# Seven products in place of eight for 31 more weight units, sums formed inside the weight buffer, and a planner that waits for whole PSUM tiles

## The chip, the cores and the metric

The kernel runs on one core of a Trainium2 chip. The metric is device microseconds of one execution, the median of several. Five engines work side by side: PE (matmuls and transposes), DVE (element-wise work on two inputs), ACT (casts, activations, copies), POOL (hardly used here) and SP, which issues the DMAs that bring the weights in.

## The reference, cut to what matters

One layer of a streaming encoder on 256 tokens of 2048 features; every large step is a product of a 256-row activation with a weight matrix read once from HBM.

```python
x = x + 0.5 * swiglu(rms_norm(x, ffn1_norm), w_gate, w_up, w_down)   # 2048 -> 5632 -> 2048
h = rms_norm(x, mix_norm); u, q, k, v, g, a = split(h @ w_in)
x = x + concat(pool_mixer(u), gated_linear_attention(q, k, v, g, a)) @ w_out
x = x + cross_attention(rms_norm(x), rms_norm(mem))                  # w_q, w_kv, then @ w_o
x = x + 0.5 * swiglu(rms_norm(x, ffn2_norm), w_gate2, w_up2, w_down2)
out = rms_norm(x) * final_norm
```

## The kernel before

**Units.** The weights come in 378 units of 1 MB (`load`, a tile `raw` of 128 x 2048 f32). Each value is split into a rounded part and the rest, so that fast matmuls keep f32 accuracy: ACT casts `raw` to `wh`, DVE subtracts to get `wl` (`split`). Activations are kept split in the same way (`xs` for the normalised input, `ys` for hidden or attention outputs). A product of two split numbers takes three matmuls: high by high, high by low, low by high.

**A plain unit** (`unit_p`, `block_t`) holds two k tiles by two column blocks of 512, and has two token halves: 8 products of three matmuls, 24 matmuls of 128 x 128 x 512. **A seven unit** (`split_seven`, `seven`) forms the same 2 x 2 block product with 7 products in Strassen's manner (21 matmuls). For that it needs sums of activation tiles (`part_sums`, once for each pair of k tiles and reused by every block; they go to `xe`), sums of the four weight pieces (DVE), a second cast and subtraction for the pieces that stand alone (`xh`, `xl`, 128 x 1536), and after the last seven unit of a block a few DVE and ACT operations that put the partial products together (`combine`, then `join`).

**Blocks.** A block is 8 units (6 for the shorter down products) that accumulate into PSUM tiles `pt`. PSUM holds four tiles of two banks each. A plain block (`block_t`) uses two tiles, a block with seven units (`block_s`) four: two hold products that `combine` reads, two the sums that `join` reads.

**Stages.** Each feed-forward network (`ffn`) runs in three parts (`FF_PARTS`): gate and up blocks (32, 32 and 24 units), transposes of the hidden rows (`turn`, tile `ph`), then the down product into x (`into_x`; 16, 16 and 12 units). Before the change seven units are used in gate and up blocks alone, at `PAIRS` (0, 2, 4, 6) of each 8, except in the very first gate block of each network: 80 units. The down products, `w_out` and `w_o` are plain, and so is the last part of the second down product (`down_end`), before and after.

**What sets the order.** The code records operations; `Plan` then gives each an estimated cost and a latest start, and lists them engine by engine (`schedule`); each engine runs its list in that order. The recorder tracks which parts of a tile an operation touches in cells of 64 elements (`grain`), so the planner takes the two banks of a PSUM tile to be independent, while the tile framework that emits the semaphores makes a writer wait for earlier readers of the whole PSUM tile. `Stream.emit` splits weights ahead of PE: by one unit for the first four units, by two after (`AHEAD`); `wh` and `wl` have three buffers, `xh` and `xl` two, `raw` three (`RAW`). The sums of weights go to a tile `T` of their own, with one buffer for each stage.

In the profile nearly every instruction has the line of the recorder's call (L469), so groups are told apart by their tiles.

Of the kernel before, what the change touches and what calls it, by code (L numbers as in the profile page):

```python
# [36 lines left out]
class Stream:  # L37
# [7 lines left out]
    RAW = 3  # L45
    FIRST = 4
# [15 lines left out]
    def unit(self, load, f, split=None, prepare=None):  # L62
        self.items.append((len(self.units), f))
        self.units.append((load, split, prepare))
        self.pending = [(n - 1, h) for n, h in self.pending]
        self._flush()

    def emit(self, load, prepare, split):
        done, w, late = -1, {}, []
        for u, f in self.items:  # L70
            if u is None:
                f()
                continue
            ahead = 1 if u < self.FIRST else self.AHEAD
            while done < min(u + ahead, len(self.units) - 1):
                done += 1
                while late:
                    late.pop(0)()
                if done + 1 < len(self.units):
                    prepare(done + 1, self.units[done + 1][2])  # L80
                w[done], rest = split(done, self.units[done][1])

                def finish(done=done, rest=rest):
                    if rest:
                        rest()
                    if done + self.RAW < len(self.units):
                        load(done + self.RAW)

                if rest:
                    late.append(finish)  # L90
                else:
                    finish()
            f(*w.pop(u))


def cost(engine, name, args, kw, writes, reads):
# [12 lines left out]
    if engine == "scalar":  # L109
# [5 lines left out]
        if "accum_out" in kw:  # L115
            busy += 0.1
# [10 lines left out]
class Buf:  # L127


    def __init__(self, shape, make, scope=None, psum=False, dtype=None):  # L130
# [6 lines left out]
        self.grain = 1 if n <= 128 else 64  # L137
# [72 lines left out]
class Task:  # L210
    __slots__ = ("i", "engine", "run", "busy", "tail", "moved", "preds", "succs", "start", "late",
                 "table", "what")
# [7 lines left out]
class Plan:  # L220
# [61 lines left out]
    def touch(self, t, v, write):  # L282
# [3 lines left out]
        b.users.append(t)  # L286
        for c in v.cells():
            spans = b.cells.setdefault(c, [])
            keep = []
            for s in spans:  # L290
                p0, p1, wrote, u = s
                if p0 < v.p1 and v.p0 < p1:
                    if write or wrote:
                        self.dep(t, u, wrote)
                    if write and v.p0 <= p0 and p1 <= v.p1:
                        continue
                keep.append(s)
            keep.append((v.p0, v.p1, write, t))
# [37 lines left out]
    def latest(self):  # L336
# [17 lines left out]
        for t in reversed(order):  # L354
            late = -t.busy - t.tail
            for s in t.succs:
                if t.engine is None:
                    x = s.late
                elif t.moved:
                    x = s.late - 1.8 - t.moved / 338e3  # L360
# [9 lines left out]
    def schedule(self):  # L370
# [47 lines left out]
        while any(waiting.values()):  # L418
# [7 lines left out]
            busy = t.busy  # L426
# [5 lines left out]
            if t.moved:  # L432
                wire = max(wire, at + 1.8) + t.moved / 338e3
# [8 lines left out]
    WAIT = 0.2  # L442

# [9 lines left out]
class Recorder:  # L453
# [3 lines left out]
    def __getattr__(self, name):  # L457
        def call(*args, **kw):
# [12 lines left out]
            t = plan.add(e, run, **cost(e, name, args, kw, writes, reads))  # L471
            t.what = (name, [v.buf.name for v in writes], [v.buf.name for v in reads])
# [8 lines left out]
def build(ctx, tc, I, out):  # L481
# [142 lines left out]
    def finish_norm(n, spread_too=True):  # L624
# [3 lines left out]
        if spread_too:  # L628
            diag["R"] = [diagonal(Rcol[:, t : t + 1]) for t in range(2)]
# [87 lines left out]
    def part_sums(act, ext, i, g):  # L717

        t = local([P, 4 * NB], F32, tag="T", name=uid("T"))
        a = t[:, :NB].rearrange("p (k s) -> p k s", k=2)  # L720
        e = t[:, NB : 2 * NB].rearrange("p (n s) -> p n s", n=4)
# [4 lines left out]
        a11, a21, a12, a22 = (a[:, k, h * P : (h + 1) * P] for k in range(2) for h in range(2))  # L726
        nc.vector.tensor_tensor(out=e[:, 3], in0=a11, in1=a21, op=ALU.subtract)
        nc.vector.tensor_tensor(out=e[:, 1], in0=a22, in1=a21, op=ALU.subtract)
        nc.vector.scalar_tensor_tensor(
            out=e[:, 2], in0=e[:, 1], scalar=-1.0, in1=a11, op0=ALU.mult, op1=ALU.subtract  # L730
        )
        nc.vector.tensor_tensor(out=e[:, 0], in0=a12, in1=e[:, 2], op=ALU.add)
        split(ext[:, i, 0], ext[:, i, 1], e)

    def add_weights(u, raw):
        t = local([P, 4 * NB], F32, tag="T", name=f"T{u}")
        w = raw.rearrange("p (b n) -> p b n", n=NB)
        v = t.rearrange("p (b n) -> p b n", n=NB)
        nc.vector.tensor_tensor(
            out=v[:, 0:2], in0=w[:, 1:3], in1=w[:, 0:1].to_broadcast([P, 2, NB]), op=ALU.add  # L740
        )
        nc.vector.tensor_tensor(out=v[:, 2], in0=v[:, 0], in1=w[:, 2], op=ALU.add)
        nc.vector.tensor_tensor(out=v[:, 3], in0=v[:, 2], in1=w[:, 3], op=ALU.add)
        return t

    def split_seven(u, raw, t):
        th, tl = (
            tile_of(wpool, [P, 4 * NB], F32R, tag=n, name=f"{n}{u}", bufs=st.AHEAD + 1)
            for n in ("wh", "wl")
        )  # L750
        split(th, tl, t)
        parts = [x.rearrange("p (b n) -> p b n", n=NB) for x in (th, tl)]

        if True:
            r = [
                local([P, 3 * NB], F32R, tag=n, name=f"{n}{u}", bufs=2)
                for n in ("xh", "xl")
            ]
            split(*r, raw[:, NB:])
            parts.extend(x.rearrange("p (b n) -> p b n", n=NB) for x in r)  # L760

        return [parts], None

    def seven(banks, act, ext, i, g, first, later, weights):
        th, tl, rh, rl = weights
        k0, k1, lo, hi = 2 * g, 2 * g + 1, slice(0, P), slice(P, S)
        a11, a12, a22 = ([act[:, k, p, t] for p in range(2)] for k, t in ((k0, lo), (k1, lo), (k1, hi)))
        n4, n1, s2, s3 = ([ext[:, i, p, n] for p in range(2)] for n in range(4))
        table = {
            "P1": (a11, rh[:, 0], rl[:, 0]), "P3": (n4, rh[:, 1], rl[:, 1]),  # L770
            "P2": (a12, rh[:, 2], rl[:, 2]), "P5": (n1, th[:, 0], tl[:, 0]),
            "P7": (s3, th[:, 1], tl[:, 1]), "P6": (s2, th[:, 2], tl[:, 2]),
            "P4": (a22, th[:, 3], tl[:, 3]),
# [3 lines left out]
        for n in order:  # L777
            (a, b), wh, wl = table[n]
            for j, (x, w) in enumerate(((a, wh), (a, wl), (b, wh))):
                nc.tensor.matmul(  # L780
                    banks[n], x, w, start=first and j == 0,
                    stop=not later and n in ("P1", "P5", "P6", "P7") and j == 2,
                )

    def block_s(srcs, act, ext, pairs, evict, delays=(0, 0), joins=(1, 0)):

        held, n = {}, len(srcs)

        def open_banks():
            a, b, c, d = (ptile(uid("pt")) for _ in range(4))  # L790
            held["ps"] = (d, c)
            held["parts"] = (a, b)
            held["banks"] = {
                "P1": a[:, 0], "P6": a[:, 1], "P7": b[:, 0], "P5": b[:, 1],
                "P2": c[:, 0], "P4": c[:, 1], "P3": d[:, 0],
            }

        def unit_s(g):
            def fn(weights):
                if g == pairs[0]:  # L800
                    open_banks()
                seven(held["banks"], act, ext, pairs.index(g), g, g == pairs[0], g != pairs[-1],
                      weights)
            return fn

        def unit_p(g):
            def fn(wh, wl):
                wh, wl = (w.rearrange("p (k j n) -> p k j n", j=2, n=NB) for w in (wh, wl))
# [3 lines left out]

# [876 lines left out]
```

## Time and profile before

| | us |
|---|---|
| median of three runs (2136.68 to 2138.38) | 2136.95 |
| the profiled execution's own time | 2133.25 |
| its span, first to last instruction | 2131.5 |
| mean granted TensorE clock | 0.997 |

How to read it: "busy" is the time in which an engine had at least one instruction under way; "idle before" and "waits" say how long an engine stood still ahead of an instruction, and who released it. Consecutive instructions of DVE and ACT overlap slightly, so the distance from one start to the next is a better price than the length of one. A stage is cut out with a window from the span's start: the second gate and up stage of the first network is 275 to 441 us, the down product after it 441 to 530, `w_o` 1324 to 1421, the first gate and up stage of the second network 1421 to 1587.

### The profile page before, as it was taken

The page shows a single profiled execution, that of the slowest core. Times are in us where ns is not written, and L with a number is a line of the kernel's source. Part 1 is how long each engine was busy: PE and PEld are TensorE (multiplying, and loading weights), DVE is VectorE, ACT ScalarE, POOL GpSimd, SP SyncE. Part 2 cuts the span into 40 slices and gives each one's busy share as a digit, 9 for nine tenths or more (in the row PEclk, how much of TensorE's full clock was granted, in tenths as well). Part 3 has the DMA queues.
Part 4 walks back from the last instruction along what each step waited for, and adds up shares of the span by engine and source line. Part 5 has one row for each costly group of instructions (what it writes and reads, how often), then busy time and mean ns, then how long its engine had stood idle before and what let it go on. Part 6 is the DMA issues. An engine that isn't in the chain of part 4 may idle for free.

```text
span 2131.5 us, 24136 instructions
## 1 busy us (share of the span) xinstructions
PE 2101.8 (99%) x9954; PEld 1754.1 (82%) x9954; DVE 1551.7 (73%) x1315; ACT 1041.7 (49%) x918; POOL 15.8 (1%) x41
## 2 busy tenths in 40 slices
PE   8999999999999999899999999999999999999998
PEld 6888888888888888788888888888888888888886
DVE  7997599966996577565556554568994899758974
ACT  6554355533554555346444444445553455435543
POOL 0000000000000000000000000000000000000001
PEclk9999999999999999999999999999999999999999
DMA  7557656566666655467655555665567655766673
GB/s 250 199 185 255 221 201 210 196 237 217 214 204 239 213 161 184 132 192 282 224 191 159 173 162 162 212 198 197 197 214 235 222 198 186 248 217 217 197 257 119
DMA packets 143318, 435.93 MB, mean 205 GB/s; under 512 B 9828, under 2 KB 13000, under 8 KB 142824
## 3 DMA queue, kind: packets, MB, share of 16 engines
q1 hardware_dynamic: 143176, 434.38, 61.0%
q8 instruction: 78, 1.28, 0.2%
q14 instruction: 32, 0.26, 0.0%
q10 hardware_dynamic: 32, 0.01, 0.0%
HBM read 417.58 MB, written 16.78 MB: 204 GB/s over the span
## 4 chain that ended last, share of the span: by engine, by line
PE 84%; DVE 9%; ACT 3%; issue 2%; DMA 2%; SPq 0%; DVEq 0%; ACTq 0%
PE pt L469 57%; PE pa L469 15%; PE pb L469 6%; DVE wl L469 4%; PE pe L469 3%; DVE T L469 2%; ACT wh L469 2%; DVE sg L469 2%; PE ph L469 1%; DVE xl L469 1%; DMA raw<-in_ffn_w_gate 1%; PE pv L469 1%; PE pl L469 1%; PE px L469 1%; DMA raw<-in_ffn_w_up 0%
## 5 line engine op out<-in xcount | busy, mean ns | idle before, releaser
L469 DVE TENSOR_TENSOR wl<-raw,wh 128x2048 fp32r<-128x2048 f32 (+2 forms) x302 | 680.8, 2255 | 425.4 <-ACT wh L469 424.6
L469 ACT CAST wh<-raw 128x2048 fp32r<-128x2048 f32 (+3 forms) x303 | 568.7, 1877 | 607.9 <-PE pt L469 367.4
L469 PE MATMUL pt<-wh,xs 128*128 128x512 f32 x1696 | 540.3, 391 | 1.8 <-ACT wh L469 1.8
L469 PE MATMUL pt<-wh,ys 128*128 128x512 f32 x1728 | 535.4, 390 | 0.0
L469 PEld LDWEIGHTS pt<-wh,ys 128*128 128x128 f32 x1728 | 324.4, 188 | 67.0
L469 PEld LDWEIGHTS pt<-wh,xs 128*128 128x128 f32 x1696 | 319.8, 189 | 68.1 <-ACT wh L469 2.0
L469 PE MATMUL pt<-wl,ys 128*128 128x512 f32 x864 | 336.2, 389 | 0.0
L469 PE MATMUL pt<-wl,xs 128*128 128x512 f32 x848 | 332.1, 392 | 1.9 <-DVE wl L469 1.1
L469 PE MATMUL pa<-xs,wh 128*128 128x512 f32 x912 | 320.1, 397 | 0.0
L469 ACT CAST wh<-T 128x2048 fp32r<-128x2048 f32 x80 | 153.2, 1915 | 255.6 <-DVE T L469 215.5
L469 PE MATMUL pa<-xs,wl 128*128 128x256 f32 x896 | 248.5, 280 | 0.0
L469 DVE TENSOR_TENSOR wl<-T,wh 128x2048 fp32r<-128x2048 f32 x80 | 183.2, 2290 | 31.5 <-ACT wh L469 31.5
L469 PEld LDWEIGHTS pa<-xs,wh 128*128 128x128 f32 x912 | 170.7, 188 | 39.6 <-issue 0.3
L469 PEld LDWEIGHTS pt<-wl,ys 128*128 128x128 f32 x864 | 162.2, 188 | 33.5
L469 PEld LDWEIGHTS pt<-wl,xs 128*128 128x128 f32 x848 | 160.2, 189 | 35.9 <-DVE wl L469 1.6
L469 PEld LDWEIGHTS pa<-xs,wl 128*128 128x128 f32 x896 | 169.1, 189 | 1.2
L469 PE MATMUL pt<-wh,xe 128*128 128x512 f32 x480 | 162.8, 390 | 0.8 <-ACT sg L469 0.8
L469 ACT CAST xh<-raw 128x1536 fp32r<-128x1536 f32 x80 | 118.4, 1480 | 49.5 <-DMA raw<-in_ffn_w_gate 28.8
L469 DVE TENSOR_TENSOR xl<-raw,xh 128x1536 fp32r<-128x1536 f32 x80 | 140.1, 1752 | 0.0
L469 PE MATMUL pb<-wh,xs 128*128 128x512 f32 x384 | 121.8, 392 | 0.0
L469 PE MATMUL pt<-xh,xs 128*128 128x512 f32 x320 | 115.2, 390 | 0.0
L469 DVE TENSOR_TENSOR T<-T,raw 128x512 f32<-128x512 f32 x160 | 110.4, 690 | 4.1
(162 smaller groups left out, 1773.7 us busy)
## 6 DMA issues: line engine op xcount, KB each, us to landing
raw<-in_ffn_w_down SPq DMA_DIRECT2D x88, 1024.0 KB, 5.5
raw<-in_ffn_w_up SPq DMA_DIRECT2D x80, 1024.0 KB, 5.1
raw<-in_ffn_w_gate SPq DMA_DIRECT2D x77, 1024.0 KB, 5.1
raw<-in_w_in SPq DMA_DIRECT2D x32, 1024.0 KB, 5.3
raw<-in_xattn_w_kv SPq DMA_DIRECT2D x32, 1024.0 KB, 5.3
raw<-in_w_out SPq DMA_DIRECT2D x16, 1024.0 KB, 6.6
raw<-in_xattn_w_q SPq DMA_DIRECT2D x16, 1024.0 KB, 5.2
raw<-in_xattn_w_o SPq DMA_DIRECT2D x16, 1024.0 KB, 5.6
```

Of the source, the lines that this page charges most:

```text
L469: return f(*(real(a) for a in args), **{k: real(a) for k, a in kw.items()})
```

## The change

1. **More seven units.** Two of each 8 (or 6) units in the down products (not in the last part), `w_out` and `w_o`, and three in the first gate block of the second network, 31 units in all by the program's order (80 casts `xh` before, 111 after). `part_sums` is now used on `ys` too (tile `ye`), and writes one of its four sums over the activation tile that it stands for. `residual` adds the two halves of such a block's result to x separately (`spare`: the combined parts from SBUF, then the PSUM sums).
2. **Sums in place.** `split_seven` first splits the pieces that stand alone, then forms the four sums inside `raw` with four additions of 128 x 512, then splits `raw`. `T` and the separate step `prepare` are gone; `raw` has four buffers; splitting runs two units ahead from the start.
3. **Planner.** A PSUM tile counts as one cell; DMAs, accumulating activations and the first matmuls are given other costs.
4. **Scopes.** `w_out` has a scope of its own, the loads of `mem` come after it, and `w_o` runs in the scope of the second network.

```diff
-    RAW = 3
-    FIRST = 4
+    RAW = 4
...
-            ahead = 1 if u < self.FIRST else self.AHEAD
-            while done < min(u + ahead, len(self.units) - 1):
+            while done < min(u + self.AHEAD, len(self.units) - 1):
                 done += 1
...
-        self.grain = 1 if n <= 128 else 64
+        self.grain = n if psum else 1 if n <= 128 else 64
...
+        lo, hi = (0, 128) if b.psum else (v.p0, v.p1)
...
-            busy = t.busy
+            busy = t.busy * (2 if e == "tensor" and at < self.SLOW else 1)
...
+    def split_seven(u, raw):
+        alone = [local([P, 3 * NB], F32R, tag=n, name=f"{n}{u}", bufs=2) for n in ("xh", "xl")]
+        split(*alone, raw[:, NB:])
         w = raw.rearrange("p (b n) -> p b n", n=NB)
-        v = t.rearrange("p (b n) -> p b n", n=NB)
-        nc.vector.tensor_tensor(
-            out=v[:, 0:2], in0=w[:, 1:3], in1=w[:, 0:1].to_broadcast([P, 2, NB]), op=ALU.add
-        )
-        nc.vector.tensor_tensor(out=v[:, 2], in0=v[:, 0], in1=w[:, 2], op=ALU.add)
-        nc.vector.tensor_tensor(out=v[:, 3], in0=v[:, 2], in1=w[:, 3], op=ALU.add)
+        nc.vector.tensor_tensor(out=w[:, 1], in0=w[:, 1], in1=w[:, 0], op=ALU.add)
+        nc.vector.tensor_tensor(out=w[:, 0], in0=w[:, 0], in1=w[:, 2], op=ALU.add)
+        nc.vector.tensor_tensor(out=w[:, 2], in0=w[:, 1], in1=w[:, 2], op=ALU.add)
+        nc.vector.tensor_tensor(out=w[:, 3], in0=w[:, 2], in1=w[:, 3], op=ALU.add)
...
+        split(*sums, raw)
...
+            held["rest"] = {j: (e[:, 0:2], ALU.add) if j else (e[:, 2:4], ALU.subtract) for j in joins}
+            if spare:
+                for j in joins:
+                    spare(j, *held["rest"][j])
...
+    DOWN_PAIRS = {16: (2, 5), 12: (2, 4)}
+    OUT_PAIRS = (3, 5)
...
-                if lo == b == 0:
+                pairs = first if lo == b == 0 else PAIRS
+                if pairs:
+                    block_s(wwide(wg, n0), xs, xe, pairs, joined_to(lambda j, c: ev_gate(j, c, 0)))
+                else:
                     block_t(wwide(wg, n0), xs, lambda j, ps: ev_gate(j, ps, 1))
...
-    into_x(I["w_out"][0], ys, 1.0, G_X)
+    into_x(I["w_out"][0], ys, 1.0, G_X, spread_too=False, pairs=OUT_PAIRS, made=1)
...
-    into_x(w_o, ys, 1.0, G_FFN2, spread_too=False)
     st.op(close_scope, 1)
     st.op(open_scope("s_ffn2"), 1)
+    into_x(w_o, ys, 1.0, G_FFN2, spread_too=False, pairs=OUT_PAIRS, made=1, then=folded)
...
-    ffn(I["ffn2_w_gate"][0], I["ffn2_w_up"][0], I["ffn2_w_down"][0], down_last)
+    ffn(I["ffn2_w_gate"][0], I["ffn2_w_up"][0], I["ffn2_w_down"][0], down_last, PAIRS[1:])
```

The first place is PE in the mixer, at the first head's `scores` (tile `pq`, matmuls on 64 partitions, between matmuls `pb` of the value projection). Before:

```order
L469 MATMUL pb_5897<-wl_5847,xs 128x512
L469 MATMUL pb_5897<-wh_5836,xs 128x512
L469 MATMUL pq_5929<-m_5590,k_5686 64x256
L469 MATMUL pq_5929<-m_5590,k_5686 64x192
L469 MATMUL pq_5929<-m_5590,k_5686 64x128 [waits DVE_49]
L469 MATMUL pq_5929<-q_5495,k_5686 64x64 [waits DVE_49]
```

Now:

```order
L456 MATMUL pb_6090<-wl_6042,xs 128x512
L456 MATMUL pb_6090<-wh_6031,xs 128x512
L456 MATMUL pq_6124<-m_5777,k_5873 64x256
L456 MATMUL pq_6124<-m_5777,k_5873 64x192
L456 MATMUL pq_6124<-m_5777,k_5873 64x128
L456 MATMUL pq_6124<-q_5682,k_5873 64x64
```

The four matmuls stay where they were; the third and fourth no longer wait for DVE's copies out of the same tile, which now all come behind them.

The second place is DVE in the second gate and up stage of the first network, one seven unit and its plain neighbour (`T` and `xl` belong to the seven unit, whose `wl` comes last). Before:

```order
L469 TENSOR_TENSOR T_1988<-raw_1933 128x1024 [waits DMAHW7_49,DVE_49]
L469 TENSOR_TENSOR wl_1996<-raw_1862,wh_1983 128x2048 [waits DMAHW5_49,Activation_49]
L469 TENSOR_TENSOR T_1988<-T_1988,raw_1933 128x512 [waits DVE_49] x2
L469 TENSOR_TENSOR xl_2017<-raw_1933,xh_1975 128x1536
L469 TENSOR_TENSOR wl_2032<-T_1988,wh_2020 128x2048 [waits Activation_49]
```

Now:

```order
L456 TENSOR_TENSOR xl_2309<-raw_2202,xh_2256 128x1536 [waits DMAHW7_49,Activation_49]
L456 TENSOR_TENSOR raw_2202<-raw_2202 128x512 [waits DVE_49] x4
L456 TENSOR_TENSOR wl_2337<-raw_2214,wh_2317 128x2048 [waits DMAHW0_49,Activation_49]
L456 TENSOR_TENSOR wl_2351<-raw_2202,wh_2339 128x2048 [waits Activation_49]
L456 TENSOR_TENSOR xl_2364<-raw_2260,xh_2305 128x1536 [waits DMAHW1_49]
```

`xl` moved ahead of the sums, each of the four sums waits for the DVE operation before it, and the plain neighbour's `wl` stands between the sums and the seven unit's `wl`.

The third place is ACT at the start of the program, around the fourth weight unit's cast (`wh_331` from `raw_194` before, `wh_252` from `raw_138` now; `j` are squares of x for the first norm). Before:

```order
L469 CAST xe_231<-T_257 128x512 [waits DVE_49]
L469 ACTIVATE j_307,ss<-x_147 128x256 [waits Activation_49]
L469 ACTIVATE j_311,ss<-x_147 128x256 [waits DMAHW0_49,Activation_49]
L469 ACTIVATE j_315,ss<-x_147 128x256 [waits Activation_49]
L469 ACT_TABLE_LOAD
L469 ACTIVATE chain<-chain 128x2 [waits DVE_49]
L469 CAST wh_331<-raw_194 128x2048 [waits DMAHW6_49]
```

Now:

```order
L456 ACTIVATE xs<-px_221,gains 128x256 [waits DVE_49]
L456 CAST wh_252<-raw_138 128x2048 [waits DMAHW4_49]
L456 ACTIVATE j_262,ss<-x_87 128x256 [waits DMAHW5_49,Activation_49]
L456 ACTIVATE j_271,ss<-x_87 128x256 [waits Activation_49]
L456 ACTIVATE xs<-px_264,gains 128x256 [waits PE_49]
```

The fourth unit's cast moved from behind all sixteen squares and the table load to a place ahead of ten of the squares; its load, which had to wait for the first unit's buffer before, has a buffer of its own now.

More of the change, by code (lines that the diff above doesn't have):

```diff
@@ L442 @@
     WAIT = 0.2
+    SLOW = 9.0
     def emit(self):
@@ L471, in call @@
             t = plan.add(e, run, **cost(e, name, args, kw, writes, reads))
+            t.f32 = e == "tensor" and name == "matmul" and args[1].dtype is F32
             t.what = (name, [v.buf.name for v in writes], [v.buf.name for v in reads])
@@ L762, in split_seven @@
[L762 to L768, printed above, removed]
+        ]
+        split(*sums, raw)
+        return [[x.rearrange("p (b n) -> p b n", n=NB) for x in (*alone, *sums)]]
```

256 lines of the change are left out of this document (131 added, 125 removed).

## The prediction

> **What bounds the kernel now.** I read the page's totals first, then the chain that ended last, then what PE waited for, then stretches by stage.
>
> ```profile
> span 2131.5 us, 24136 instructions
> PE 2101.8 (99%) x9954; PEld 1754.1 (82%) x9954; DVE 1551.7 (73%) x1315; ACT 1041.7 (49%) x918; POOL 15.8 (1%) x41
> PE 84%; DVE 9%; ACT 3%; issue 2%; DMA 2%; SPq 0%; DVEq 0%; ACTq 0%
> ```
>
> PE is the bound: busy for 99% of the span and 84% of the chain. DVE is the only other engine on the chain worth the name. What a matmul costs is read from an unbroken piece of the chain, since matmuls overlap their neighbours:
>
> ```profile
> 193.21 157.78 PE pt L469 x696
> ```
>
> 157.78 / 696 = 0.2267 us for each 128 x 128 x 512 matmul. A plain unit's 24 take 5.44 us, a seven unit's 21 take 4.76. What PE waits for, by releaser, with total, times and longest:
>
> ```profile
> PE pq L469 <- DVE ST L469: 4.0, 8, 0.6
> PE pgain L469 <- DMA gain<-in_ffn_norm: 3.8, 1, 3.8
> ...
> PE pt L469 <- ACT sg L469: 1.6, 3, 0.8
> PE pb L469 <- ACT v L469: 1.6, 2, 0.8
> ...
> PE pt L469 <- DVE wl L469: 1.1, 1, 1.1
> ```
>
> Few and small: weights and DMAs are ahead of PE nearly everywhere. How much room DVE has differs by stage (columns: stretch, its length, then busy time of PE, PEld, DVE, ACT, POOL with instructions, clock, DMA share, GB/s):
>
> ```profile
> 275.00:441.00 166.00, 165.26 (x737) 136.49 (x736) 156.66 (x117) 89.14 (x61) 0.00 (x0) 1.00 0.61 209
> 441.00:530.00 89.00, 89.00 (x402) 73.98 (x401) 52.52 (x33) 35.21 (x20) 0.00 (x0) 1.00 0.64 225
> 1324.00:1421.00 97.00, 97.00 (x449) 81.04 (x448) 49.25 (x32) 42.93 (x44) 0.00 (x0) 1.00 0.63 202
> 1421.00:1587.00 166.00, 165.05 (x742) 136.08 (x742) 150.98 (x137) 91.82 (x73) 0.00 (x0) 1.00 0.60 199
> ```
>
> In gate and up stages DVE is busy 156.7 of 166 us, 94%; in the down product and `w_o` little over half. The change puts DVE work into both.
>
> **Term 1, matmuls removed.** The program's order has 31 more seven units, not 35 (23 in the two networks, 8 in `w_out` and `w_o`). Each saves 3 matmuls: 93 x 0.2267 = 21.1 us, all on the bounding engine. Transposes stay.
>
> **Term 2, whole PSUM tiles.** The four matmuls of `scores` wait for DVE's copies between them, 8 times, 4.0 us; in the new order those two waits of each head are gone. The waits of `pb` for ACT `v` (1.6) and of `pt` for ACT `sg` (1.6) are of the same kind: an eviction placed after the first bank's last matmul holds up the second bank's. By the planner's new rule a read of a tile comes behind all its matmuls. Sum 7.2 us. Bounds: 4.0 if only the shown place counts, 9 if the restarts cost something too. The other side of it, copies that come later, lies beside the next unit's 5.4 us of matmuls. I take 7.2.
>
> **Term 3, the start.** PE's timeline (start, length, then the wait before it):
>
> ```profile
> 26.69 1.03 PE L469 MATMUL px<-ident,x 128*128 128x128 f32 x8
> 29.50 1.20 PE L469 MATMUL pt<-wh,xs 128*128 128x512 f32 x4 [1.78 <-ACT wh L469]
> 31.83 0.79 PE L469 MATMUL pt<-wl,xs 128*128 128x512 f32 x1 [1.13 <-DVE wl L469]
> 32.42 0.63 PE L469 MATMUL pt<-wh,xs 128*128 128x512 f32 x1
> 32.85 0.63 PE L469 MATMUL pt<-wl,xs 128*128 128x512 f32 x1
> 33.27 1.05 PE L469 MATMUL pt<-wh,xs 128*128 128x512 f32 x2
> 34.13 0.63 PE L469 MATMUL pt<-wl,xs 128*128 128x512 f32 x1
> 34.55 0.91 PE L469 MATMUL pt<-wh,xs 128*128 128x512 f32 x2
> 35.30 0.39 PE L469 MATMUL pt<-wl,xs 128*128 128x512 f32 x1
> ```
>
> PE stands 1.78 + 1.13 us for the fourth unit, then its next 8 matmuls take 35.30 - 31.83 = 3.47 us in place of 8 x 0.2267 = 1.81: 1.7 more. Sum 4.6 us. Now this unit's load has a fourth buffer and its cast stands ahead of ten squares, so I count 4.5 gained. Bounds: the gain is 0 if the next unit is late in its place; it is a loss of 3 if the x pieces, now behind 1 MB more on SP's queue, come late (at the mean rate below 1 MB is 5 us, with one unit, 5.4 us, of cover).
>
> ```profile
> DMA packets 143318, 435.93 MB, mean 205 GB/s; under 512 B 9828, under 2 KB 13000, under 8 KB 142824
> ```
>
> The Trainium skill has the slow matmuls in "TensorE: Matmul & The Clock Gate", section "What's actually happening": half clock after about 3.4 us of idleness. By it the pauses here, 1.8 and 1.1 us, would slow nothing and this term would be 2.9; the trace has matmuls 0.43 us apart behind them, so the row decides.
>
> **Term 4, DVE's new work.** DVE's timeline inside 275 to 441 us, a plain and a seven unit:
>
> ```profile
> 323.60 2.28 DVE L469 TENSOR_TENSOR wl<-raw,wh 128x2048 fp32r<-128x2048 f32 x1
> 325.80 1.22 DVE L469 TENSOR_TENSOR T<-raw 128x1024 f32<-128x1024 f32 x1
> 327.05 1.42 DVE L469 TENSOR_TENSOR T<-T,raw 128x512 f32<-128x512 f32 x2
> 328.39 1.75 DVE L469 TENSOR_TENSOR xl<-raw,xh 128x1536 fp32r<-128x1536 f32 x1
> 330.53 2.29 DVE L469 TENSOR_TENSOR wl<-T,wh 128x2048 fp32r<-128x2048 f32 x1 [0.39 <-ACT wh L469]
> 332.86 1.22 DVE L469 TENSOR_TENSOR T<-raw 128x1024 f32<-128x1024 f32 x1
> ...
> L469 DVE TENSOR_TENSOR T<-T,raw 128x512 f32<-128x512 f32 x160 | 110.4, 690 | 4.1
> L469 DVE TENSOR_TENSOR sg<-pt,sg 128x1024 f32<-128x1024 f32 x60 | 72.9, 1221 | 2.2 <-PE pt L469 1.3
> L469 DVE SCALAR_TENSOR_TENSOR x<-pt,x 128x1024 f32<-128x1024 f32 x28 | 34.1, 1221 | 0.7
> L469 DVE TENSOR_TENSOR T<-T 128x128 f32<-128x128 f32 x24 | 6.3, 286 | 0.2
> ...
> L469 ACT CAST wh<-T 128x2048 fp32r<-128x2048 f32 x80 | 153.2, 1915 | 255.6 <-DVE T L469 215.5
> L469 ACT CAST xh<-raw 128x1536 fp32r<-128x1536 f32 x80 | 118.4, 1480 | 49.5 <-DMA raw<-in_ffn_w_gate 28.8
> ```
>
> The plain `wl` holds DVE 2.20 us (323.60 to 325.80). An operation that waits for the one before starts about 0.03 after its end, one that doesn't 0.08 before: so the two sums of 0.69 take 0.73 + 0.61. The seven unit took 2.59 (sums) + 1.67 (`xl`) + 2.20 (`wl`) = 6.46 busy, and 0.39 waiting for ACT's cast. Now: 1.67, 0.12 because the first sum waits for `xl`, sums 3 x 0.73 + 0.61 = 2.80, `wl` 2.20: 6.79. The cast (1.9) lies beside the neighbour's `wl`, so the 0.39 goes. An old seven unit thus costs 0.33 more busy time and about nothing in elapsed time; a new one costs 6.79 - 2.20 = 4.59.
>
> Gate and up, 275 to 441: 16 x 0.33 = 5.3, DVE 162.0 of 166. The down product: 4 x 4.59 = 18.4; two `combine` (1.22 + 2 x 0.69 = 2.6) 5.2; four additions to x, 4.9; two `part_sums` (one of 0.69, four of 0.29, and two subtractions of 128 and 384 columns, by size some 0.8 together: 2.65) 5.3. Sum 33.8: 52.5 + 33.8 = 86.3, in a stretch that shrinks from 89 to 89 - 12 x 0.2267 = 86.3. Both together 248.3 of 252.3 us, 98%. The two neighbouring stretches of the second network: 1421 to 1587 gets 12 x 0.33 + 3 x 4.59 + 2.6 + two joins 2.4, less one `part_sums` that moves ahead: 171.1 of 166 - 2.0 = 164.0. **There DVE has 7 us more to do than PE.** `w_o` ahead of it has room (49.3 + 33.8 of 94), so DVE enters with its full lead: `wl` is finished up to two units, 10.9 us, less cast and subtraction (1.9 + 2.2) and their hand-over, before PE needs it: some 6 us, an estimate.
>
> At 98% not every wait is hidden. I charge 6 us: about 2 in that stage and under 1 in each of the other five gate and up stages and the first network's last down product. Bounds: 0 if the lead covers all; 14, twice the 7, if the lead is used up by the evictions that stand at the end of each block.
>
> **At nothing:** more casts on ACT (31 x 1.5 us on an engine at 49%); the new scopes (`w_o`'s first seven unit is its fourth, 16 us after the stage starts, against one `values` eviction to wait for); the later `mem` loads (first needed 12 units of `w_q` later); `T`'s successor sharing a buffer with the squares. Without that cover each costs a few us once. SP's order changes by the fourth buffer only.
>
> **Sum.** -21.1 - 7.2 - 4.5 + 6 = -26.8 against the profiled execution's 2133.25 us: 2106.5. The median of the runs stands 3.7 above that execution, so **2110**.
>
> **Rivals.** *DVE is no bound after all* (chance 0.15): its lead hides term 4, or the sums' waits cost nothing, 0.12 x 444 = 53 us less DVE work: 2110 - 6 = 2104. For it: in all of before PE waited 1.1 us in one place for `wl`. Against it: 171.1 of 164. The Trainium skill is on its side: "VectorE: DVE Perf Modes", section "The DRAIN you can't avoid", has chained operations take equally long with a semaphore after each or only after the last. The rows above, 0.03 after against 0.08 before, disagree.
>
> *DVE becomes the bound of both networks* (0.11): the 0.39 stays, for old and new, because ACT's cast is late behind its other casts: 111 x 0.39 = 43 us of DVE, less some 4 us of room in each of five gate-and-down pairs: 23 us lost, 2110 + 23 = 2133, within 0.2% of before; with half of it 2121.
>
> *Slower* (0.06): the in-place sums, read and written in the same tile, cost more than 0.73. It decides where DVE's excess eats the 27 us gained and the 20 of room: 47 / 444 = 0.11 us each. At 0.12 more over that point, 0.23 each, 102 - 47 = 55 us is lost: 2192; just beyond it, at 0.13 each, 2148. Against it: sums in place of 128 x 128 stand in the rows at 0.29 like others of their size.
>
> *The change does less than it says* is counted already: 35 units would save 105 matmuls, 2.7 us more.
>
> **Chances and range.** The forecast's own case 0.68: its terms give 2101 (gains of 23 to 31, term 4 at 0 to 4) to 2122 (term 3 lost, term 4 at 10 to 14). The first rival lies within. I give **2101 to 2126**, which takes half of the second rival; what is outside is below 0.2. A measurement of this kernel can tell about 0.2% (4.3 us) from no change. Faster 0.91: the forecast, the first rival, most of the second. Same 0.03: the rest of it. Slower 0.06.
>
> **What would show it.** After: matmuls in a piece of the chain still 0.2267 apart; no wait of `pq` for `ST`; no pause at 27 to 32 us; DVE near 98% in gate and up stages, with PE's waits for `wl` in the first stage of the second network. Wrong if the chain there goes over to DVE for long pieces, or if PE pauses at new places: the seams of down products, whose blocks now need all four PSUM tiles.

## The result, and the profile after

The changed kernel takes 2122.16 us, the median of four runs (2121.56 to 2125.00); the kernel before took 2136.81 beside it (2133.23 to 2138.38). The ratio is 0.9936, its 95% interval 0.9919 to 0.9954: 14.65 us faster, where 27 were forecast. The profiled execution took 2122.68 us, 10.6 less than the one profiled before.

The page's totals and the shares of the chain that ended last, after:

```profile
span 2120.8 us, 24464 instructions
PE 2089.4 (99%) x9861; PEld 1732.5 (82%) x9861; DVE 1799.5 (85%) x1731; ACT 1102.5 (52%) x1002; POOL 15.8 (1%) x41
PE 54%; DVE 34%; issue 6%; ACT 3%; DMA 2%; SPq 0%; DVEq 0%; ACTq 0%
```

93 matmuls are gone, as the order had said. But DVE, 9% of the chain before, is now 34% of it. What PE waited for (total, times, longest), its matmuls first, then the costliest row of its weight loads:

```profile
PE pt L456 <- DVE wl L456: 8.6, 19, 1.5
PE pt L456 <- DVE sg L456: 5.0, 5, 1.1
PE px L456 <- DMA x<-in_x: 4.5, 2, 4.1
PE pt L456 <- ACT xs L456: 2.0, 1, 2.0
...
PEld pt L456 <- DVE wl L456: 25.8, 45, 1.9
```

The rows of `pq`, `pb`, `pp` and `ps` have left the list. The wait of PE's matmuls for weights (`wl`) has grown from one of 1.1 us to 19, and waits for DVE's evictions of PSUM (`sg`) are new. Windows of four stages (columns as before: length, then busy time of PE, PEld, DVE, ACT, POOL): the first network's second gate and up stage, `w_o`, the second network's first and third gate and up stages. DVE is busy for 96, 98 and 93% of the three gate and up windows.

```profile
270.00:439.00 169.00, 166.93 (x735) 135.40 (x734) 161.82 (x138) 90.89 (x63) 0.00 (x0) 1.00 0.58 205
1308.00:1397.00 89.00, 89.00 (x413) 74.40 (x413) 77.39 (x76) 47.82 (x47) 0.00 (x0) 1.00 0.68 223
1397.00:1572.00 175.00, 170.61 (x755) 137.61 (x755) 171.24 (x173) 102.96 (x91) 0.00 (x0) 1.00 0.58 196
1915.00:2044.00 129.00, 126.77 (x553) 103.42 (x552) 120.42 (x100) 64.45 (x42) 0.00 (x0) 0.99 0.60 205
```

Where time came from and went is best read by stage, from PE's first matmul of one stage to its first of the next. The table has the same reading for experiments told below; each column is one profiled execution. Left out are the other down products, which go like down 1 (88.8 us before, 86.6 to 86.8 after), and the cross-attention ahead of `w_o` (295.7 and 295.2).

| stage, us | before | after | e1 tiles alone | e5 three sums | e9 told | e14 both | e10 own tile | e13 |
|---|---|---|---|---|---|---|---|---|
| network 1, gate and up 1 | 178.3 | 176.8 | 179.3 | 176.6 | 174.4 | 174.3 | 173.9 | 176.0 |
| down 1 | 88.8 | 86.5 | 88.8 | 87.0 | 86.3 | 86.1 | 86.4 | 86.4 |
| gate and up 2 | 166.1 | 169.6 | 167.7 | 170.0 | 170.8 | 165.8 | 166.3 | 166.3 |
| gate and up 3 | 125.6 | 127.7 | 125.5 | 127.3 | 125.6 | 124.9 | 124.2 | 124.1 |
| down 3 | 68.1 | 68.5 | 68.1 | 68.9 | 68.6 | 66.0 | 66.2 | 66.1 |
| mixer | 216.5 | 204.6 | 204.6 | 204.6 | 204.7 | 204.7 | 204.6 | 204.7 |
| `w_out` | 88.8 | 86.2 | 88.9 | 86.1 | 86.1 | 86.1 | 86.1 | 86.1 |
| `w_o` | 91.7 | 89.0 | 91.7 | 89.0 | 89.0 | 89.0 | 89.0 | 89.0 |
| network 2, gate and up 1 | 171.2 | 175.3 | 170.5 | 173.5 | 178.0 | 170.3 | 175.9 | 170.0 |
| gate and up 2 | 166.2 | 169.6 | 167.7 | 169.8 | 169.5 | 167.0 | 166.3 | 166.3 |
| gate and up 3 | 124.4 | 129.1 | 126.6 | 127.4 | 125.9 | 124.9 | 124.2 | 124.2 |

Gained: 11.9 us in the mixer, 5.9 up to the sixth unit of the start (its first matmul stands at 37.95 us, 43.87 before), 2 to 2.7 in each product of the new units but one. Lost: 2 to 5 us in nearly every gate and up stage. Matmuls, mixer and start together give 21.1 + 11.9 + 5.9 = 38.9, and 10.6 is left of it: some 28 us were lost (24 by the medians of the runs), about 23 of them in the gate and up stages and 5 in the products of the new units. Not all of it need come from the sums: e1, which has neither sums in place nor new units, stands 5.5 us longer over the six gate and up stages than the kernel before.

### The profile page after: what moved, and what is told of

Same layout as the page of the kernel before. It is cut to its first block, busy times and chain, and to the rows that moved or that the text cites. A ratio compares the mean times of both kernels' runs of the same rounds, so it can differ in the third digit from the quotient of the medians.

```text
span 2120.8 us, 24464 instructions
## 1 busy us (share of the span) xinstructions
PE 2089.4 (99%) x9861; PEld 1732.5 (82%) x9861; DVE 1799.5 (85%) x1731; ACT 1102.5 (52%) x1002; POOL 15.8 (1%) x41
## 4 chain that ended last, share of the span: by engine, by line
PE 54%; DVE 34%; issue 6%; ACT 3%; DMA 2%; SPq 0%; DVEq 0%; ACTq 0%
PE pt L456 27%; PE pa L456 15%; DVE wl L456 14%; DVE raw L456 8%; PE pb L456 6%; DVE xl L456 5%; DVE sg L456 5%; PE pe L456 3%; ACT wh L456 3%; DMA raw<-in_ffn_w_gate 1%; DVE ys L456 1%; DMA raw<-in_ffn_w_up 1%; DVE T L456 1%; DVE x L456 1%; PE pv L456 1%
## 5 line engine op out<-in xcount | busy, mean ns | idle before, releaser
L456 ACT CAST wh<-raw 128x2048 fp32r<-128x2048 f32 (+2 forms) x383 | 718.4, 1885 | 630.8 <-DVE raw L456 323.5
L456 DVE TENSOR_TENSOR wl<-raw,wh 128x2048 fp32r<-128x2048 f32 (+2 forms) x382 | 856.7, 2258 | 198.6 <-ACT wh L456 197.6
L456 PE MATMUL pt<-wh,xs 128*128 128x512 f32 x1820 | 590.4, 391 | 6.5 <-DVE sg L456 4.5
L456 PE MATMUL pt<-wh,ys 128*128 128x512 f32 x1392 | 441.3, 390 | 0.0
L456 DVE TENSOR_TENSOR raw<-raw 128x512 f32<-128x512 f32 x444 | 306.8, 691 | 13.4
L456 PEld LDWEIGHTS pt<-wh,ys 128*128 128x128 f32 x1392 | 261.2, 188 | 54.7 <-issue 0.2
L456 PE MATMUL pt<-wl,ys 128*128 128x512 f32 x696 | 271.2, 390 | 0.5 <-DVE wl L456 0.5
L456 PEld LDWEIGHTS pa<-xs,wh 128*128 128x128 f32 x912 | 170.8, 188 | 39.8 <-issue 0.7
L456 DVE TENSOR_TENSOR xl<-raw,xh 128x1536 fp32r<-128x1536 f32 x111 | 194.3, 1750 | 9.3 <-ACT xh L456 9.1
L456 DVE TENSOR_TENSOR sg<-pt,sg 128x1024 f32<-128x1024 f32 (+1 forms) x147 | 140.8, 966 | 9.9 <-ACT sg L456 7.0
L456 PEld LDWEIGHTS pb<-wh,xs 128*128 128x128 f32 x384 | 72.1, 188 | 15.2 <-issue 0.3
```

The source lines that it names most:

```text
L456: return f(*(real(a) for a in args), **{k: real(a) for k, a in kw.items()})
```

## The experiments

Differences are to the kernel before, timed beside each run (medians of 2133.5 to 2133.6). The changed kernel's own is -14.7, with the kernel before at 2136.8 beside it, and it was not timed again beside the others. So a comparison with the changed kernel is open by some 3 us: by the times alone, without the differences, each run below stands that much better against it.

| run | median | difference | ratio, 95% interval |
|---|---|---|---|
| e1 whole PSUM tiles alone, on before | 2123.74 | -9.8 | 0.9953 (0.9939 to 0.9968) |
| e2 without the 31 new units | 2128.32 | -5.2 | 0.9975 (0.9965 to 0.9986) |
| e4 a fifth sum | 2160.64 | +27.1 | 1.0125 (1.0109 to 1.0140) |
| e5 three sums | 2118.88 | -14.7 | 0.9930 (0.9915 to 0.9945) |
| e7 two sums in one, in place | 2115.14 | -18.4 | 0.9916 (0.9901 to 0.9931) |
| e8 three raw buffers | 2144.99 | +11.5 | 1.0056 (1.0041 to 1.0071) |
| e9 planner told of waits | 2119.34 | -14.2 | 0.9935 (0.9920 to 0.9950) |
| e10 sums in a tile of their own | 2100.89 | -32.6 | 0.9849 (0.9833 to 0.9866) |
| e11 as e10, raw tile held | 2115.34 | -18.3 | 0.9907 (0.9890 to 0.9923) |
| e12 as e10, uncounted 0.36 us | 2127.32 | -6.3 | 0.9964 (0.9951 to 0.9977) |
| e13 as e10, plain first gate | 2095.49 | -38.1 | 0.9819 (0.9804 to 0.9834) |
| e14 three sums and told | 2097.76 | -35.8 | 0.9831 (0.9815 to 0.9848) |

**e1 and e2: parts of the change alone.** e1 is the kernel before with these lines of the planner's:

```diff
-        self.grain = 1 if n <= 128 else 64
+        self.grain = n if psum else 1 if n <= 128 else 64
...
+        lo, hi = (0, 128) if b.psum else (v.p0, v.p1)
```

> The kernel before with one part of the change alone: the planner takes a PSUM tile as one cell. Theory A (the parts add up, the middle stages gain what the trace after shows there): the mixer shortens by about 12 us, from 216.5 to 204.6, nothing else moves, 2136.8 - 12 = 2125 (2122 to 2128). Rival 1 (the listed waits alone, as predicted): 2136.8 - 7.2 = 2129.6. Rival 2 (the mixer's gain comes from the fourth raw buffer or from the earlier start, not from the order): 2136.8.

2123.7, in theory A's range. The mixer takes 204.6 us, as in the changed kernel: this part alone does it. Not all of it stays: three gate and up stages lose 1.5 to 2.2 us. PE waits there for an eviction `sg` at a block change (5 waits, 4.8 us in all). PE's timeline of e1 at such a place:

```profile
318.65 0.39 PE L470 MATMUL pt<-xh,xs 128*128 128x512 f32 x1
320.16 0.50 PE L470 MATMUL pt<-xh,xe 128*128 128x512 f32 x1 [1.13 <-DVE sg L470]
```

e2 takes the new units out of the changed kernel:

```diff
-    DOWN_PAIRS = {16: (2, 5), 12: (2, 4)}
-    OUT_PAIRS = (3, 5)
+    DOWN_PAIRS = {16: (), 12: ()}
+    OUT_PAIRS = ()
...
-    ffn(I["ffn2_w_gate"][0], I["ffn2_w_up"][0], I["ffn2_w_down"][0], down_last, PAIRS[1:])
+    ffn(I["ffn2_w_gate"][0], I["ffn2_w_up"][0], I["ffn2_w_down"][0], down_last)
```

> The changed kernel without its 31 new units of seven products (the down products, the output products and the first gates of the second network stay with plain units), so 93 matmuls of 0.2267 us more. Theory A (the sums of the new units cost nothing in the down and output products and cost more than they save in the first gates of the second network): six of these products lose 2.2 to 2.7 us each, the third one of the first network nothing, the first stage of the second network gains about 1.4; 2122.2 + 12.7 = 2135 (2132 to 2138). Rival 1 (the matmuls count in full): 2122.2 + 21.1 = 2143. Rival 2 (new units are worth nothing, since VectorE bounds everything): 2122.

In it the activation sums of the second network stand ahead of the plain first gate block, which then multiplies blocks already overwritten by sums. The 31 units are worth 14.7 - 5.2 = 9.5 us of their 21.1 (6.2 by the times alone), less than theory A's 2132 to 2138 for this run would make them. By the profiles of the two kernels, the new units save about 14 us in the down and output products, and 8 of it go again: each of the six gate and up stages is shorter by 0.8 to 2.5 us without them, though only one of the six holds any of the new units.

**e4 and e5: more and less of DVE's work.** In each of 111 units, e4 makes the fourth sum twice, and e5 leaves it out. The edit of e4:

```diff
         nc.vector.tensor_tensor(out=w[:, 3], in0=w[:, 2], in1=w[:, 3], op=ALU.add)
+        nc.vector.tensor_tensor(out=w[:, 3], in0=w[:, 2], in1=w[:, 3], op=ALU.add)
```

> The changed kernel with one sum more in each of the 111 units of seven products (the last 128x512 sum is made twice over, so its result is another): 111 x 0.725 = 80 us more of VectorE. Theory A (VectorE bounds the gate and up products, where 83 of the 111 units are, and stands close to it in the down products): 83 x 0.725 = 60 us more at least, and up to 75; 2182 to 2197. Rival 1 (the sums' chain of waits holds raw tiles too long, and VectorE's sum of work is no bound): the units are longer by 0.7 us in a chain that runs beside others, under 10 us, 2122 to 2132.

> The changed kernel without the last of the four sums in each of the 111 units (one product of seven then multiplies a raw block in place of the sum): 111 x 0.6 to 0.7 = 67 to 77 us less of VectorE. Theory A: the gate and up products come back to the matmuls' time, all of the roughly 28 us lost there returns and no more, since the matmuls bound from there on; 2122 - 28 = 2094 (2090 to 2102). Rival 1 (loads that come late through raw tiles held by the sums): only the 0.6 us per unit by which raw tiles come free earlier, of which next to nothing shows; 2117 to 2122.

Both missed theory A, the bare sum of DVE's work. 80 us more cost 42 (27.1 + 14.7), and some 70 us less gave back between nothing and 3 us. e4's time stands between its two theories. e5's lies in the range of its rival 1, loads that come late; e11 and e14 below take that up. DVE's busy time in e5 is 1730.8 us for 1799.5, and yet its second gate and up stage takes 170.0 us, and PE still waits for `wl` (rows below). So the work can be made smaller without the stall going away.

**What is in the rows of a seven unit.** DVE's timeline after, two units of a steady pair:

```profile
317.02 1.75 DVE L456 TENSOR_TENSOR xl<-raw,xh 128x1536 fp32r<-128x1536 f32 x1
318.81 2.87 DVE L456 TENSOR_TENSOR raw<-raw 128x512 f32<-128x512 f32 x4
321.60 4.48 DVE L456 TENSOR_TENSOR wl<-raw,wh 128x2048 fp32r<-128x2048 f32 x2
326.00 1.75 DVE L456 TENSOR_TENSOR xl<-raw,xh 128x1536 fp32r<-128x1536 f32 x1
```

A pair takes 326.00 - 317.02 = 8.98 us of DVE, less than the 10.2 of its matmuls (24 + 21). Inside it, `xl` takes 1.79 to the next start and the four sums 2.79: each of the first four of these five operations is followed by a wait of 0.12. The planner's rule (`ready`) is that an operation on the same engine starts with the earlier one's issue unless it reads what that one writes. The fourth sum reads the third: that wait is counted. But the first sum overwrites what `xl` reads, the second what the first reads, the third what the second reads. These three waits, 0.35 us a unit, stand in the trace and not in the plan; with sums in a tile of their own there was nothing to overwrite. Theory B was that the stall comes from them.

**e9: the planner told.** No instruction differs, only the order.

```diff
-            elif p.engine == t.engine and not p.moved and (p.engine == "tensor" or not data):
+            elif p.engine == t.engine and not p.moved and (p.engine == "tensor" or not data and p.engine != "vector"):
                 x = p.start + p.busy
...
-                elif s.engine == t.engine and (t.engine == "tensor" or not s.preds[t]):
+                elif s.engine == t.engine and (t.engine == "tensor" or not s.preds[t] and t.engine != "vector"):
```

> The changed kernel with one thing told to its planner: that on VectorE an instruction which overwrites what an earlier one reads starts only after that one's end. No instruction is added or left out. Theory B: the plan then counts the 0.35 us per unit and puts evictions and splits where they are due; part of the roughly 28 us comes back by order, 2116 (2108 to 2121); the work itself stays. Rival D (the order does not matter, VectorE's work does): 2122, or worse by a bad order, to 2128.

-14.2: no difference from the changed kernel. The time, 2119.3, stands in theory B's range, but only by the 3 us that are open. Three stages shrink by 2 to 3 us, two grow by 1 to 3. Taken alone, this run doesn't bear theory B out.

**e10 and e7: fewer waits.** e10 puts the sums back into a tile of their own, by three operations, with three raw buffers:

```diff
-    RAW = 4
+    RAW = 3
...
+        t = tile_of(wpool, [P, 4 * NB], F32, tag="T", name=f"T{u}")
+        v = t.rearrange("p (b n) -> p b n", n=NB)
+        nc.vector.tensor_tensor(
+            out=v[:, 0:2], in0=w[:, 1:3], in1=w[:, 0:1].to_broadcast([P, 2, NB]), op=ALU.add
+        )
+        nc.vector.tensor_tensor(out=v[:, 2], in0=v[:, 0], in1=w[:, 2], op=ALU.add)
+        nc.vector.tensor_tensor(out=v[:, 3], in0=v[:, 2], in1=w[:, 3], op=ALU.add)
...
-        split(*sums, raw)
+        split(*sums, t)
```

> The changed kernel with the sums in a tile of their own again, by three instructions as before the change, and so with three raw buffers (the fourth's space holds that tile). Theory B: no in-place wait, 0.3 to 0.4 us less of VectorE per unit: the gate and up stages come to what the kernel before with whole PSUM tiles alone showed (167.7, 125.5, 167.7, 126.6 us for 169.6, 127.7, 169.6, 129.1), the second network's first stage to about 172; 2122 - 12 = 2110 (2104 to 2116). Rival C (the fourth raw buffer is what carries the new units, three are too few): 2122 or slower. Rival D (VectorE's bare work): 2119 to 2122.

18 us faster than the changed kernel, more than expected. Its DVE timeline:

```profile
309.59 1.21 DVE L456 TENSOR_TENSOR T<-raw 128x1024 f32<-128x1024 f32 x1
310.84 1.42 DVE L456 TENSOR_TENSOR T<-T,raw 128x512 f32<-128x512 f32 x2
312.18 1.75 DVE L456 TENSOR_TENSOR xl<-raw,xh 128x1536 fp32r<-128x1536 f32 x1
314.30 2.29 DVE L456 TENSOR_TENSOR wl<-T,wh 128x2048 fp32r<-128x2048 f32 x1 [0.37 <-ACT wh L456]
316.50 2.28 DVE L456 TENSOR_TENSOR wl<-raw,wh 128x2048 fp32r<-128x2048 f32 x1
318.71 1.22 DVE L456 TENSOR_TENSOR T<-raw 128x1024 f32<-128x1024 f32 x1
```

The pair takes 318.71 - 309.59 = 9.12 us here, no less than in place, because DVE waits for ACT's cast; without that wait it is 8.75. e7 stays in place, but one 128x1024 operation makes the first two sums, so that two uncounted waits and one operation go (seven units' raw blocks are loaded in the order 1, 2, 3, 0 for it, in more and smaller loads):

```diff
+        nc.vector.tensor_tensor(
+            out=w[:, 0:4:3], in0=w[:, 3:4].to_broadcast([P, 2, NB]), in1=w[:, 0:2], op=ALU.add
+        )
+        nc.vector.tensor_tensor(out=w[:, 1], in0=w[:, 0], in1=w[:, 1], op=ALU.add)
+        nc.vector.tensor_tensor(out=w[:, 2], in0=w[:, 1], in1=w[:, 2], op=ALU.add)
```

> The changed kernel, still with its sums in place, but the first two sums made by one instruction over 128x1024 (the raw blocks are loaded in a turned order, so that it may overwrite two of them): three instructions for four, and one wait less or two. Theory B (what costs the time are the in-place waits that the planner does not know of: 0.11 us where the first sum overwrites what the split before it still reads, 0.12 where the second overwrites what the first reads, 0.12 on the third, some 0.35 us of drift per unit, until the matrix engine waits): two of three waits go, 0.3 us of VectorE per unit; the gate and up stages lose less, 2112 (2106 to 2117). Rival D (a bare sum of VectorE's work, of which 0.6 us per unit left out gave back only 3 us before): 1 to 2 us, 2119 to 2121.

-18.4: 3.7 us better than the change, a fifth of what e10 gives. The time, 2115.1, is within theory B's range, but the gain is short of the 10 us that its 2112 stood for. So a third theory was to be heard: sums in place also hold the raw tile through cast and second split (theory C).

**e8 and e11: the raw tile.** e8 is the changed kernel with `RAW = 3`. e11 is e10 with a small copy that holds each seven unit's raw tile to the end of its split:

```diff
         split(*sums, t)
+        z = tile_of(wpool, [P, 1], F32, tag="z", name=f"z{u}")
+        nc.scalar.activation(z, f32(sums[1][:, 0:1]), AF.Copy, scale=raw[:, 0:1])
```

> The changed kernel with three raw buffers again in place of four. Theory B: the sums' waits are the same; a raw tile of a seven unit is held from its load through the sums to the second split, so some loads come later; 2122 to 2135. Rival C (the raw ring bounds already with four: a load starts only when the unit four before has left its raw tile, and lands 5.1 us later): with three the ring turns in three units where its 20.4 us now cover four, which is some 5 us for each pair of units in the gate and up stages; over 2200.

> The version with the sums in a tile of their own and three raw buffers (2100.9 us), but each seven unit's raw tile is kept until its second split is done, as sums in place keep it: a copy of one column on ScalarE that reads the raw tile and the finished split (111 more ScalarE instructions, nothing more on VectorE). Theory C (what costs the 21 us between sums in place and sums apart is that the raw tile is held through sums, cast and second split, some 4 us longer, so that loads come late): like the kernel with sums in place and three raw buffers, less its waits, 2125 to 2145. Theory B (VectorE's own waits of 0.12 us in the in-place sums, which the planner does not count): 2101 to 2106.

With three buffers, holding costs 14.3 us (e11 against e10; the 111 small copies on ACT are part of that). With the sums in place, taking the fourth buffer away costs 26.2 (e8 against the change; 22.8 by the times alone). Both runs missed both theories: they are faster than theory C's price for e8 and its range for e11, and slower than theory B's ranges. The holding clearly costs with three buffers, and the fourth buffer is needed if the sums stand in raw.

**e12: the waits without the holding.**

```diff
         nc.vector.tensor_tensor(out=v[:, 3], in0=v[:, 2], in1=w[:, 3], op=ALU.add)
+        nc.vector.tensor_tensor(out=v[:, 3, :160], in0=v[:, 3, :160], in1=w[:, 3, :160], op=ALU.add)
...
     if engine == "vector":
+        if name == "tensor_tensor" and writes[0].at.size == 160:
+            return dict(busy=0.0, tail=-0.153)
```

> The version with the sums in a tile of their own and three raw buffers (2100.9 us), with one more add of 128x160 behind the last sum of each seven unit, which waits for that sum: 0.12 of wait and 0.24 of work by the rows of the other sums, 0.36 us per unit, set to nothing in the planner's costs (one product's sum gets a block twice). It gives VectorE what the sums in place have in waits and leaves the raw tiles free early. Theory B (unplanned 0.35 us per unit on VectorE): most of the 21 us comes back, 2112 to 2122. Theory C (raw tiles held): nearly nothing, 2101 to 2106.

2127.3: 26.3 us for 111 x 0.36 = 40 us of DVE that the plan does not have, more than theory B expected. Its chain shows DVE as the changed kernel's does:

```profile
PE 54%; DVE 32%; issue 7%; ACT 5%; DMA 2%; ACTq 0%; DVEq 0%; SPq 0%
```

What e12 doesn't part is the added time itself from its not being counted. The last run does that from the other side.

**e14: e5 and e9 together,** four raw buffers, sums in place.

> The changed kernel, sums in place and four raw buffers, with both edits that alone gave back next to nothing: the last of the four sums left out in each seven unit (one product multiplies a raw block in its place), and the planner told that on VectorE an overwriting instruction waits for the reader before it. Theory B (work and unplanned waits together: left out alone, the planner fills the time and the drift stays; told alone, the plan is honest but VectorE's work no longer fits beside the matmuls): both causes are gone, 2100 to 2106. Theory C (the raw tile held through the sums costs by itself with four buffers as well): 2112 to 2118, as each edit alone.

2097.8: 21 us faster than the change, where each edit alone gave next to nothing. e5 and e14 differ in the order alone, and e14 is 21.1 us faster, with each of the six gate and up stages 2.3 to 4.2 us shorter. That is more regular than the shifts of e9, whose other order made some stages shorter and others longer. The rows of PE's weight loads waiting for `wl`, first e5, then e14:

```profile
PEld pt L456 <- DVE wl L456: 17.8, 24, 1.7
```

```profile
PEld pt L456 <- DVE wl L456: 7.3, 16, 1.3
```

And the shares of the chain that ended last, of e5, of e9 and of e14:

```profile
PE 67%; DVE 22%; ACT 4%; issue 4%; DMA 3%; SPq 0%; DVEq 0%; ACTq 0%
```

```profile
PE 75%; DVE 18%; ACT 3%; issue 2%; DMA 2%; SPq 0%; DVEq 0%; ACTq 0%
```

```profile
PE 84%; DVE 11%; issue 2%; ACT 2%; DMA 1%; SPq 0%; DVEq 0%; ACTq 0%
```

In e14 the chain is PE's again, 84% as before the change. So the stall has two causes, and each is enough by itself: the order, made without the waits for overwriting, and the work, too much for a plan that counts them. (The edit makes the plan count that wait wherever VectorE overwrites, not only in the sums; no run parts the three waits of a seven unit from the rest.) Holding the raw tile costs nothing that shows once there are four buffers and both causes are gone, so theory C doesn't explain the changed kernel by itself. But leaving out the fourth sum also frees each raw tile some 0.6 us sooner, and no run parts that from the work. Why telling alone (e9) loses in two stages what it wins in three stays open.

**e13: a version that beats both kernels.** e10 with the second network's first gate block plain again:

```diff
-    st.op(lambda: gate_sums(PAIRS[:1]), 1)
-    ffn(I["ffn2_w_gate"][0], I["ffn2_w_up"][0], I["ffn2_w_down"][0], down_last, PAIRS[1:])
+    st.op(lambda: gate_sums(PAIRS), PAIRS[-1] + 1)
+    ffn(I["ffn2_w_gate"][0], I["ffn2_w_up"][0], I["ffn2_w_down"][0], down_last)
```

> The version with the sums in a tile of their own, without the three new seven units in the second network's first gate products (3 x 3 matmuls of 0.2267 us more), whose sums are then made behind that block as in the first network. Theory A (these units cost VectorE more than they save the matrix engine: the stage took 175.9 us here, 170.5 in the kernel before with whole PSUM tiles): the stage falls to 170.5, 2100.9 - 5.4 = 2095.5 (2094 to 2098). Rival (the stage's loss is of the block change, not of these units): plus 2.0 for the matmuls, 2103.

As expected: the stage takes 170.0 us for 175.9, though it has 9 matmuls more, and the kernel 2095.5, 1.8% less than before the change.

## Why the prediction was right in sign and range, and 12 us short

The forecast was 2110 in a range of 2101 to 2126; the time is 2122.2. That it lies in the range is in part luck. With the loss in term 4 as it came, 24 to 28 us for 6, and the other terms as forecast, the sum gives 2128 to 2132, outside the range; terms 2 and 3 gained 6 us more than forecast and brought it back. By its steps:

- **Term 1, 21.1 us: right as a count of PE's work.** Six of the seven products with four new units gain 2.0 to 2.7 us where 12 matmuls make 2.72; the first network's last one gains nothing (68.5 us for 68.1). The three units of the first gate block earn nothing either (e13 against e10): there term 4 takes more.
- **Term 2, 7.2 us with bounds 4 to 9: too small.** Of the 7.2, the rows in the mixer are 5.6. The mixer gained 11.9, and e1 shows that the order of the PSUM tiles alone does it. PE's rows, which the prediction summed, leave out what the weight load waits. The view's PEld rows in that window of the kernel before:

```profile
PEld pq L469 <- DVE ST L469: 5.7, 7, 1.0
PEld pb L469 <- ACT v L469: 2.4, 2, 1.2
PEld pp L469 <- ACT ys L469: 1.5, 2, 0.8
PEld pq L469 <- ACT wh L469: 1.1, 1, 1.1
PEld ps L469 <- DVE m L469: 1.0, 1, 1.0
PEld px L469 <- ACT xs L469: 0.8, 1, 0.8
```

  They sum to 12.5, near the 11.9 gained. The prediction also left `pp`, `ps` and `px` out. On the other side it took copies that come later as hidden beside the next unit's matmuls. They were not: e1 has 4.8 us of waits for `sg`, and its whole gain is 9.8.
- **Term 3, 4.5 us: right, and a little more.** 5.9, of which 1.0 is an earlier first matmul (e1 has that too). The pause at 27 to 32 us is gone, and the x pieces behind 1 MB more held up nothing there. The order does it without the fourth buffer that the prediction counted on: in e10, with three, the sixth unit starts at 38.55 us.
- **Term 4, the failed step.** DVE's load was sized well: 161.8 us in the second gate and up stage for a forecast of 162.0, 171.24 for 171.1 in the second network's first, and a unit of 8.98 - 2.20 = 6.78 for 6.79. What failed is "At 98% not every wait is hidden. I charge 6 us", with its bound of 14: 24 to 28 us were lost, and also in stages where DVE's sum was below PE's. A sum over a stage says whether the work fits, not whether a fixed order lets it. The prediction had priced the three waits as DVE's time and not asked whether the plan counts them. e14 against e5 (the same instructions, 21 us) and e10 (nearly the same DVE time for a pair, 18 us) show that the uncounted waits together with the load make up most of the loss.

Of the rivals, *DVE is no bound* gave 2104 and fell. *DVE becomes the bound of both networks* named the right engine, and its half way, 2121, is nearly the time, by chance: its mechanism, a wait of 0.39 for ACT's cast in every seven unit, isn't there. In the steady pair above DVE doesn't wait for ACT at all, and in the whole second gate and up stage it does so 4 times, 4.7 us, beside 15 seven units. *Slower* needed sums at over 0.73 + 0.11 each; they cost 0.73 at most. By the Trainium skill, "VectorE: DVE Perf Modes", section "The DRAIN you can't avoid", a semaphore after each of a chain of copies costs nothing extra. Here an operation that waits starts 0.03 us after the end of the one before and one that doesn't 0.08 ahead of it, and an added 0.36 us a unit, of which a third is that wait, cost 26 us (e12).

Of the signs, three came true: no wait of `pq`, no pause at the start, PE waiting for `wl`. DVE's share in the gate and up windows is 93 to 98% where 98 was named. And the sign named for a wrong forecast came too: the chain went over to DVE.

## What to carry to other kernels

A plan that sets each engine's order must count every wait that a rewrite brings in: working in place makes an operation wait for the earlier reader of what it overwrites, on the same engine too (0.12 us for each here), and beside a DVE that is over 90% busy a few tenths of a microsecond left out per unit cost about as much as the 93 matmuls saved (21 us, e14 against e5). Where leaving out work changes nothing, and mending the plan changes nothing, try both at once before either theory is dropped. And price the removal of a matmul's wait by the rows of its weight load.

## What was not expected of the hardware

PE fell to half speed after two short pauses, shorter than those at the start of the kernel before (1.78 and 1.13 us). PE's timeline after, in the second network's third gate and up stage:

```profile
1956.19 0.39 PE L456 MATMUL pt<-wh,xs 128*128 128x512 f32 x1
1957.15 0.50 PE L456 MATMUL pt<-xh,xs 128*128 128x512 f32 x1 [0.58 <-DVE sg L456]
1957.49 0.40 PE L456 MATMUL pt<-xl,xs 128*128 128x512 f32 x1
1957.72 0.40 PE L456 MATMUL pt<-xh,xs 128*128 128x512 f32 x1
1959.23 0.64 PE L456 MATMUL pt<-wh,xs 128*128 128x512 f32 x1 [1.11 <-DVE sg L456]
1959.66 0.63 PE L456 MATMUL pt<-wl,xs 128*128 128x512 f32 x1
1960.09 0.63 PE L456 MATMUL pt<-wh,xs 128*128 128x512 f32 x1
```

Waits of 0.58 and 1.11 us, with three matmuls between, and from 1959.23 on matmuls stand 0.43 us apart for 3.4 us; the granted clock is 0.76 over 1956 to 1963 us and 1.00 in the 6 us ahead. The pauses cost 0.74 + 1.28 us, the slow matmuls behind them another 1.6 (eight at 0.43 in place of 0.23). The Trainium skill, "TensorE: Matmul & The Clock Gate", section "What's actually happening", has the drop after an idle window of about 3.4 us. The trace, which decides here, has it after two pauses that together are 2 us, and a recovery after 3.4.
